# Gates and branch projections with tokens as rows, a DeltaNet inverse from 16-wide blocks, and a list schedule made in six passes

## The chip, the core and the metric

The kernel runs on one core of a Trainium2 chip. The metric is the time of one launch in microseconds of the device; lower is better. Five engines work side by side, each through a list of instructions of its own: TensorE (PE; its weight loads are shown apart as PEld), VectorE (DVE), ScalarE (ACT), GpSimd (POOL) and SyncE (SP), which here only issues DMA transfers.

## What is computed

Two layers over 256 tokens of width 1024. Each layer, cut to what matters here:

```python
h = rms_norm(x, norm_g)
proj = h @ w_in                        # qa ka va za ba aa | ub zb | qc kc vc zc iq ik iw | gates
ya = deltanet_branch(...)              # conv, silu, gated delta rule in chunks, per-head norm, silu(za)
yb = pooling_branch(ub, zb, pool_w, pool_scale)
yc = sparse_attention_branch(...)      # indexer scores, top 64 keys per query, softmax
projected = einsum('btnc,ncd->btnd', stack([ya, yb, yc]), w_branch)       # three of 512 x 1024
gate = sigmoid(gates.reshape(b, t, 3, 1024) + gate_b)
x = x + sum(gate * projected, axis=branch) @ w_out
```

Inside the DeltaNet branch a unit lower triangular matrix is inverted for each chunk and head (`triangular_solve(eye + lmat, eye)`). All is float32.

## The kernel before, in words

**Precision.** A float32 product is made of three products in the fp32r format: a weight block arrives by DMA in a buffer `raw` (4 of them), ACT casts it to `wh` (6 buffers), DVE subtracts to get `wl` (6 buffers), and TensorE adds up wh with hh, wh with hl and wl with hh, where hh and hl are the two parts of the normalised input. `wslot` (from line 576) does this for a block of 128 x 1024 numbers, so every block costs a DMA on SP, about a microsecond of ACT and 1.2 us of DVE.

**Projections.** `proj_cm` makes channels the rows of the result: the weights stand in TensorE, 256 tokens move past, 24 products of 128x256 per half bank. It serves the gates, the conv inputs and the silu paths. `proj_tm` makes tokens the rows: the activations stand and 512 weight columns move; it serves q, k and v of the attention. The results go to the PSUM banks `pj` (4 of them); `mx` (4 more) take the rest. The branch projections use the weights as stationary too, 256 tokens moving: the inner loops `for p in range(4)` after `acc`.

**Gates.** For each of the three branches four `proj_cm` of 256 channels, then ACT makes tanh with the bias `hb` of each channel's partition into a tile `tg`; DVE multiplies the branch product with it and adds into `acc`. `mh` and `ml`, the two parts of the sum, are the stationary side of the out-projection (`outp`, the first KOUT=2 of 8 row blocks for all output pieces, then the others piece by piece).

**Inverse.** `uc` holds the eight 32-wide diagonal blocks of both chunks and four heads. In 31 rounds DVE shuffles a row of `xi` into `xb`, multiplies and adds. Then TensorE joins 32-wide to 64-wide and 128-wide blocks with small products (p1, p2, p3), whose results ACT and DVE copy back.

**Order of the work.** Nothing is issued as it is written. Class `Plan` records every operation; `lay_out` is a list scheduler that walks through time with an estimated cost for each (`cost`), takes for each engine the ready operation of the smallest `prio` (the place in the program plus `plan.shift`: LATE, X1, CRIT and BACK are such shifts), and assigns buffers. `emit` then issues the list, so every instruction has one line in the profile, L454. The engines follow this list strictly in order on the chip.

**Parameters.** At the start and again at each layer SP issues small DMAs: `heads`, the norm gains, and into a tile `f` gate biases, conv weights, pool scales and one norm gain (77 rows), which TensorE transposes to channels as rows. `rsqrt` is a power on POOL (`rs` for the input norm, `r4k` and `r4q` for the attention's keys and queries, `rk`, `so` for the DeltaNet). After the input norm TensorE transposes `big` (the normalised x) and ACT and DVE make hh and hl from it.

Of the kernel before, what the change touches and what calls it, by code (L numbers as in the profile page):

```python
# [30 lines left out]
for _n, _c in (("ident", 128), ("upper", 128), ("supper", 128), ("strict", 128), ("bd", 128),  # L31
               ("ncaus", 128), ("eye32", 32), ("cosa", 128), ("sina", 128), ("cosi", 64),
               ("sini", 64), ("rcount", 64)):
    CST[_n] = (_w, _w + _c)
    _w += _c
CSTW = _w

NPAR = 77


LATE, X1, CRIT, BACK = 200, 132, ((-600, 60), (-600, -500)), 2000

KOUT = 2
NWARM = 40

# [3 lines left out]

PATIENCE = 600.0  # L50
NRAW, NSPL, NU, RU, WU, RB, RM, WM = 4, 6, 15, 3, 4, 1, 1, 6
# [4 lines left out]
def constants():  # L56
# [13 lines left out]
    put("eye32", (p % 32) == np.arange(32)[None, :])  # L70
# [58 lines left out]
class Tag:  # L129
    def __init__(self, phys, reserve, window, psum):  # L130
        self.phys, self.reserve, self.window, self.psum = phys, reserve, window, psum
        self.free = [(0.0, i) for i in range(len(phys))]
        self.order, self.next, self.parked, self.masks = [], 0, [], {}


class PTile:
    def __init__(self, tag):
        self.tag, self.slot, self.log, self.left, self.end = tag, None, [], 0, 0.0
        self.rank = None


class Op:
    __slots__ = ("eng", "call", "args", "kw", "cost", "tail", "prio", "port", "deps", "outs", "tiles", "wait", "est",
                 "start", "end", "n", "other", "turn", "weight")
# [24 lines left out]
class Plan:  # L169
# [3 lines left out]
    def __init__(self, tc):  # L173
        self.tc, self.nc, self.ops, self.shift = tc, tc.nc, [], 0
        nc = self.nc
        self.real = {"PE": nc.tensor, "DVE": nc.vector, "ACT": nc.scalar, "POOL": nc.gpsimd, "SP": nc.sync}
# [28 lines left out]
    def cost(self, eng, call, args, kw):  # L205
# [4 lines left out]
        if call == "dma_start":  # L210
            run = int(args[1].shape[-1]) * 4
            rate = 120.0 if run < 512 else 262.0 if run < 1024 else 318.0 if run < 4096 else 338.0
            return 475.0, n * out.shape[0] * 4 / rate, False
        if eng == "PE":
# [5 lines left out]
            if k <= 32:  # L220
                return 54.0, 170.0, False
            return 2 * (max(n, m) * (2.0 if k > 64 else 1.6) / 2.4 + 3), 170.0, False
# [10 lines left out]
        if eng == "POOL":  # L233
            if kw.get("op") == ALU.pow:
                return 400.0 + 155 * n, 40.0, True
# [18 lines left out]
    def add(self, eng, call, args, kw, other=None):  # L254
# [6 lines left out]
        o.prio, o.outs, o.est, o.start = o.n + self.shift, [], 0.0, None  # L261
# [21 lines left out]
        for t in o.tiles:  # L283
            if t.rank is None:
                t.rank = len(t.tag.order)
                t.tag.order.append(t)
        self.ops.append(o)
        return o

    def lay_out(self):  # L290
        import heapq

        for o in self.ops:
            o.wait = len(o.deps)
            for d in o.deps:
                d.outs.append(o)
            for t in o.tiles:
                t.left += 1
        engines = list(self.real)
        free = {e: 0.0 for e in engines}  # L300
        free["PE"] = 1000.0
# [4 lines left out]
        clock = Clock()  # L306
# [15 lines left out]
        def ready(o):  # L322
            at = slots(o)
            if at is not None:
                for e in [o.eng] + ([o.other[0]] if o.other else []):
                    heapq.heappush(soon[e], (max(o.est, at), o.prio, o.n, o.turn))
# [4 lines left out]
        def held(o, e):  # L331
            return o.other[2] if o.other and e == o.other[0] else o.cost

# [3 lines left out]
        def pick(e):  # L337
# [10 lines left out]
            if not now[e]:  # L348
# [4 lines left out]
                t, q = soon[e][0][0], soon[e][0][1:]  # L353
                if e in shared and uses(self.ops[q[1]], e):
                    t = max(t, shared["POOL" if e == "DVE" else "DVE"])
                return t, e, q
            if e not in shared:
                return t, e, now[e][0]
            blocked = shared["POOL" if e == "DVE" else "DVE"]
            q = now[e][0]  # L360
            if blocked <= t or not uses(self.ops[q[1]], e):
                return t, e, q
            room = blocked - t + SLACK
            for q2 in heapq.nsmallest(12, now[e]):
                if live(q2) and not uses(self.ops[q2[1]], e) and held(self.ops[q2[1]], e) <= room:
                    return t, e, q2
            return max(t, blocked), e, q
# [5 lines left out]
        while len(order) < len(self.ops):  # L373
# [20 lines left out]
            if max(got, o.est) > at + 1e-6:  # L394
# [4 lines left out]
                heapq.heappush(soon[e], (max(got, o.est), o.prio, o.n, o.turn))  # L399
# [3 lines left out]
            for t in o.tiles:  # L403
                if t.slot is None:
# [3 lines left out]
                    t.slot = f[1]  # L408
                    while g.next < len(g.order) and g.order[g.next].slot is not None:
                        g.next += 1  # L410
                    if g.free:
                        again, g.parked = g.parked, []
                        for p in again:
                            ready(p)
            o.start = at
            if e == "PE":
                free[e] = clock.run(at, o.cost, o.args[0].shape[0] * o.args[1].shape[0] / 16384.0)
# [5 lines left out]
            if o.call == "dma_start":  # L423
                dma_free = max(dma_free, at + 1360.0) + o.tail
# [24 lines left out]
    def emit(self):  # L449
# [3 lines left out]
        for o in self.lay_out():  # L453
# [5 lines left out]
def trunk(ctx: ExitStack, tc: tile.TileContext, x, norm_g, w_in, gate_b, conv_w, a_log, dt_bias, dn_onorm,  # L459
# [58 lines left out]
    cs = make("cs", [128, CSTW], F32)  # L518
# [5 lines left out]
    DMA.dma_start(x_sb[:, 1, :], x[0, 128:256, :])  # L524
    plan.shift = LATE
    DMA.dma_start(cs[:, 128:], cst[:, 128:])
# [7 lines left out]
    def brow(src_ap, n, name):  # L534
        t = make(name, [128, n], F32)
        DMA.dma_start(t, bass.AP(tensor=src_ap.tensor, offset=src_ap.offset, ap=[[0, 128], [1, n]]))
        return t

    heads = make("heads", [128, 2, 2, 4], F32)
    for i, a in enumerate((a_log, dt_bias)):  # L540
        DMA.dma_start(heads[:, i], bass.AP(tensor=a.tensor, offset=a.offset, ap=[[0, 128], [4, DEPTH], [1, 4]]))
    qkb = [brow(a, DEPTH * 128, n) for n, a in (("qn", q_norm), ("kn", k_norm))]
    qkn = [[b[:, l * 128:(l + 1) * 128] for b in qkb] for l in range(DEPTH)]
# [8 lines left out]
    sgr = make("sgr", [128, 128], F32R)  # L552
    V.tensor_copy(sgr, con("strict"))
# [13 lines left out]
    for i in range(2):  # L567
        G.memset(kiT[i], 0.0)

# [4 lines left out]
    def wslot(src, shape):  # L574
# [3 lines left out]
        for dst, s in ([(rv, src)] if not isinstance(src, list) else [(rv[:, :, a:b], s) for a, b, s in src]):  # L578
# [6 lines left out]
                lo[:, :n].rearrange("p (k c) -> p k c", k=shape[0]))  # L585

    for l in range(DEPTH):
# [12 lines left out]
        for t in range(2):  # L600
# [3 lines left out]
            ss = small(2, "ss")  # L604
            S.activation(fill(), xt[:, lo_], AF.Square, scale=1.0 / 32, accum_out=ss[:, 0:1])
            V.scalar_tensor_tensor(fill(), xt[:, hi_], 1.0 / D, xt[:, hi_], op0=ALU.mult, op1=ALU.mult,
                                   accum_out=ss[:, 1:2])
            se, rs = small(1, "se"), small(1, "rs")
# [8 lines left out]
            S.activation(xs[:, hi_], xg[:, hi_], AF.Copy, scale=rs)  # L617
# [17 lines left out]


        plan.shift = LATE
        rows = fill()[:, :128]
        DMA.dma_start(rows[0:24], gate_b[l].rearrange("i (r c) -> (i r) c", c=128))
        DMA.dma_start(rows[24:72], conv_w[l].rearrange("j (r c) -> (j r) c", c=128))  # L640
        DMA.dma_start(rows[72:76], pool_scale[l].rearrange("(r c) -> r c", c=128))
        DMA.dma_start(rows[76:77], dn_onorm[l:l + 1, :])
        pp = bank("mx")
        PE.transpose(pp[:, :NPAR], rows[:NPAR, :], ident[:NPAR, :NPAR])
        plan.shift = 0
        pt = make("pt", [128, NPAR], F32)
        S.copy(pt, pp[:, :NPAR])
        hb = make("hb", [128, 29], F32)
        V.tensor_scalar(hb[:, 0:24], pt[:, 0:24], 0.5, None, op0=ALU.mult)
        V.tensor_scalar(hb[:, 24:29], pt[:, 72:77], 0.5, None, op0=ALU.mult)  # L650
        tabs = []
        for i in range(2):
            c_t = make(f"tc{i}", [128, 2, 128], F32)
            s_t = make(f"ts{i}", [128, 2, 128], F32)
            for dst, name in ((c_t, "cosa"), (s_t, "sina")):
                tr = con(name).rearrange("p (t d) -> p t d", t=2)
                for t in range(2):
                    G.tensor_tensor(dst[:, t].rearrange("p (a d) -> p a d", a=2),
                                    tr[:, t, None, :].to_broadcast([128, 2, 64]),
                                    qkn[l][i].rearrange("p (a d) -> p a d", a=2), op=ALU.mult)  # L660
            tabs.append((c_t, s_t))
# [48 lines left out]
        def attend(which, c0):  # L710
            banks = proj_tm(c0)
            for t in range(2):
# [14 lines left out]
                rope(banks[t], t, tabs[0 if which == "q" else 1], ro)  # L727
# [189 lines left out]
        for which, c0, pr in (("k", KA, 0), ("q", QA, 0), ("k", KA, 1), ("q", QA, 1), ("v", VA, 0), ("v", VA, 1)):  # L917
# [3 lines left out]
            for b in range(2):  # L921
                blk = c0 // 128 + pr * 2 + b
                wc = [pt[:, 24 + j * 12 + blk:25 + j * 12 + blk] for j in range(4)]
# [18 lines left out]
        plan.shift = BACK  # L942
        ybh = make("y", [128, 4, T], F32R)
# [27 lines left out]
        for pr in range(2):  # L971
# [6 lines left out]
            for b in range(2):  # L978
                g = pr * 2 + b
                V.scalar_tensor_tensor(v2(y)[:, b], v2(ps)[:, b], hb[:, 24 + g:25 + g], zb[:, g], op0=ALU.mult,  # L980
# [3 lines left out]
        za = zgate(ZA)  # L984
# [9 lines left out]
        for c in range(2):  # L994
# [12 lines left out]
            if c == 0:  # L1007
# [4 lines left out]
                V.tensor_tensor(v4(kd), v4(ps), eg[:, 8:12, None].to_broadcast([128, 4, 128]), op=ALU.mult)  # L1012
# [25 lines left out]

        xi = make("xi", [128, 8, 32], F32)
        xb = make("xb", [128, 8, 32], F32)  # L1040
        V.tensor_copy(xi, con("eye32")[:, None, :].to_broadcast([128, 8, 32]))
        for r in range(31, 0, -1):
            n = 32 - r
            V.stream_shuffle(xb[:, :, r:], xi[:, :, r:], [r] * 32)
            V.tensor_tensor(xb[:, :, r:], xb[:, :, r:], uc[:, :, r:r + 1].to_broadcast([128, 8, n]), op=ALU.mult)
# [197 lines left out]
```

## Time and profile before

| | |
|---|---|
| median of 3 runs | 593.06 us (592.9 to 594.93) |
| the profiled execution's own time | 593.53 us |
| its span in the profile | 591.4 us |
| busy share of PE, DVE, ACT, POOL | 97%, 84%, 51%, 6% |
| mean granted clock of TensorE | 0.994 |
| moved by DMA | 95.66 MB, mean 162 GB/s |

The span is the time from the first to the last instruction; the rest of the execution's own time lies around it. A matmul's shown duration includes its way through the array, and the next one starts long before it ends, so what a stream of products costs is read from the distance between starts: the time of a stretch over the number of products in it. Idle time of an engine other than PE matters only where PE waits for it.

### The profile page before, as it was taken

The numbers are of one execution on the slowest core, as the hardware profiler recorded it, in microseconds if no ns is written. First come the engines' busy times: TensorE is split into PE (matmuls) and PEld (weight loads), VectorE is DVE, ScalarE is ACT, GpSimd is POOL, SyncE is SP. The second block draws the span as 40 slices with busy tenths as digits, with TensorE's granted clock in tenths as the row PEclk, the third lists the DMA queues.
The fourth block names the chain that finished last, engine by engine and source line by source line (L and its number), as shares of the span: only waits on it lengthen the run. The fifth ranks groups of instructions, "written<-read, shape, count | busy, mean of one in ns | idle before, by whom it ended". The sixth has DMA issues, their size and how long they took to land.

```text
span 591.4 us, 11398 instructions
## 1 busy us (share of the span) xinstructions
PE 575.8 (97%) x4423; PEld 546.5 (92%) x4423; DVE 495.7 (84%) x1122; ACT 301.3 (51%) x577; POOL 33.1 (6%) x36
## 2 busy tenths in 40 slices
PE   8899999999999999999989999999999999999997
PEld 6687999999899989999868879999999999999986
DVE  5899999999989975857587999999999998477571
ACT  6564376565365435545255635865554544435430
POOL 1011000011000021000011010000100002000000
PEclk9899999999999999999998999999999999999999
DMA  7662375676598653475445518927729865265511
GB/s 273 201 182 71 94 199 142 172 200 175 141 257 240 184 143 81 135 248 169 118 126 184 144 50 216 248 58 189 203 55 243 237 192 167 68 173 191 189 40 71
DMA packets 137313, 95.66 MB, mean 162 GB/s; under 512 B 5514, under 2 KB 128172, under 8 KB 137260
## 3 DMA queue, kind: packets, MB, share of 16 engines
q1 hardware_dynamic: 137260, 94.95, 56.5%
q8 instruction: 34, 0.56, 0.4%
q14 instruction: 19, 0.16, 0.1%
HBM read 93.89 MB, written 1.05 MB: 161 GB/s over the span
## 4 chain that ended last, share of the span: by engine, by line
PE 70%; DVE 19%; DMA 6%; ACT 2%; issue 2%; SPq 1%; ACTq 0%; DVEq 0%
PE pj L454 56%; PE mx L454 13%; DVE wl L454 5%; DVE u L454 5%; DMA raw<-in_w_in_dram 4%; DVE score L454 3%; DMA heads<-in_dt_bias_dram 1%; DVE top L454 1%; ACT wh L454 1%; SPq L454 1%; DVE y L454 1%; DVE big L454 1%; ACT u L454 0%; ACT hh L454 0%; DVE z L454 0%
## 5 line engine op out<-in xcount | busy, mean ns | idle before, releaser
L454 ACT CAST wh<-raw 128x1024 fp32r<-128x1024 f32 (+2 forms) x171 | 178.5, 1047 | 178.2 <-PE pj L454 86.1
L454 DVE TENSOR_TENSOR wl<-raw,wh 128x1024 fp32r<-128x1024 f32 (+1 forms) x174 | 210.3, 1214 | 36.4 <-ACT wh L454 35.1
L454 PE MATMUL pj<-hl,wh 128*128 128x256 f32 x832 | 120.8, 284 | 0.0
L454 PE MATMUL pj<-hh,wl 128*128 128x256 f32 x832 | 119.2, 284 | 1.5 <-DVE wl L454 1.5
L454 PE MATMUL pj<-hh,wh 128*128 128x256 f32 x832 | 120.6, 285 | 0.0
L454 PEld LDWEIGHTS pj<-hh,wl 128*128 128x128 f32 x832 | 107.8, 192 | 2.0 <-DVE wl L454 1.9
L454 PEld LDWEIGHTS pj<-hl,wh 128*128 128x128 f32 x832 | 108.7, 192 | 0.3
L454 PEld LDWEIGHTS pj<-hh,wh 128*128 128x128 f32 x832 | 108.5, 192 | 0.5
L454 PE MATMUL pj<-y,wh 128*128 128x256 f32 x384 | 54.7, 284 | 0.0
L454 PEld LDWEIGHTS pj<-y,wh 128*128 128x128 f32 x384 | 49.6, 192 | 0.2 <-DVE f L454 0.2
L454 PE MATMUL pj<-wh,hh 128*128 128x512 f32 (+1 forms) x128 | 38.7, 388 | 2.1 <-ACT hh L454 1.8
L454 PE MATMUL pj<-wh,hl 128*128 128x512 f32 (+1 forms) x128 | 39.0, 388 | 0.3 <-DVE hl L454 0.3
L454 PE MATMUL pj<-wl,hh 128*128 128x512 f32 (+1 forms) x128 | 37.7, 382 | 0.0
L454 PE MATMUL mx<-wh,y 128*128 128x512 f32 (+1 forms) x128 | 37.6, 377 | 0.0
L454 PE MATMUL mx<-u,u 128*128 128x128 f32 (+2 forms) x336 | 33.8, 249 | 1.2 <-DVE u L454 1.1
L454 PEld LDWEIGHTS mx<-u,u 128*128 128x128 f32 (+2 forms) x336 | 31.3, 165 | 2.5 <-DVE u L454 1.3
L454 DVE SCALAR_TENSOR_TENSOR u<-pj,pt,u 128x254 f32<-128x254 f32 (+2 forms) x72 | 31.3, 473 | 0.6 <-ACT u L454 0.6
L454 PE MATMUL pj<-y,wl 128*128 128x256 f32 x192 | 30.8, 283 | 0.0
L454 PEld LDWEIGHTS pj<-wh,hh 128*128 128x128 f32 x128 | 23.3, 192 | 6.6 <-ACT hh L454 2.4
L454 PEld LDWEIGHTS pj<-wh,hl 128*128 128x128 f32 x128 | 23.6, 193 | 5.1 <-DVE hl L454 1.4
L454 ACT COPY u<-mx 128x512 f32<-128x512 f32 (+2 forms) x30 | 12.6, 424 | 30.6 <-PE mx L454 25.9
L454 PEld LDWEIGHTS pj<-wl,hh 128*128 128x128 f32 x128 | 23.7, 194 | 4.2 <-DVE wl L454 0.2
(193 smaller groups left out, 688.6 us busy)
## 6 DMA issues: line engine op xcount, KB each, us to landing
raw<-in_w_in_dram SPq DMA_DIRECT2D x128, 512.0 KB, 4.5
raw<-in_w_branch_dram SPq DMA_DIRECT2D x24, 512.0 KB, 3.4
raw<-in_w_out_dram SPq DMA_DIRECT2D x16, 512.0 KB, 3.5
raw<-in_w_in_dram SPq DMA_DIRECT2D x4, 486.0 KB, 4.8
x_sb<-in_x_dram SPq DMA_DIRECT2D x2, 512.0 KB, 4.3
out_dram<-x_sb SPq DMA_DIRECT2D x3, 256.0 KB
raw<-in_w_in_dram SPq DMA_DIRECT2D x2, 324.0 KB, 4.1
cs<-in_cst_dram SPq DMA_DIRECT2D x1, 560.0 KB
```

Of the source, the lines that this page charges most:

```text
L454: getattr(self.real[o.eng], o.call)(*[put(a) for a in o.args], **{k: put(v) for k, v in o.kw.items()})
```

## The change

Five things change together.

1. *Gates and branch projections with tokens as rows.* `by_token` keeps a 128x128 block of hh, hl or of a branch's output standing and moves 512 weight columns, for two token blocks in turn, into two `pj` banks. A gate's bias now varies along the row, so `spread` loads it by a DMA that repeats one row to all 128 partitions (12 of 128x512), DVE adds it, and ACT makes tanh. The sum has tokens as rows, so 16 transposes per layer turn it for the out-projection.
2. *The inverse from 16-wide blocks.* 15 rounds instead of 31 on DVE, of up to 120 columns; then one more join on TensorE: `joined`, 32 products of 32x32 over the four row bands in turn, twice per layer.
3. *The schedule in passes.* `plan` lays the list out six times and keeps the shortest by its own reckoning. After each pass `deadlines` works out for each operation how late it may end without holding up TensorE in the order just found, and the other engines then rank by that time; TensorE keeps the program's rank. New rules: `SWITCH` and `REST` keep groups of small products apart, a small product is reckoned at 12 instead of 54 ns, an engine is kept off a PSUM bank that another is reading, some operations may not `begin` before a time.
4. *Parameter loads.* Conv weights, pool scales and norm gain of both layers are loaded once at the start and transposed once (128x106); these, `heads`, `qn`, most constants and `sgr` go through POOL's queue instead of SP's. SP issues the first weight block second.
5. *Constants of the order.* KOUT 2 to 4, BACK 2000 to 300, X1 and CRIT by a little; the gate `za` is made after the DeltaNet chain (`gated`); two DVE multiplications (`kd` and `rv`) go to ACT, in four pieces each.

```diff
-LATE, X1, CRIT, BACK = 200, 132, ((-600, 60), (-600, -500)), 2000
-KOUT = 2
+LATE, X1, CRIT, BACK = 200, 138, ((-600, 0), (-600, -500)), 300
+KOUT = 4
+SWITCH = 90.0
+REST = 2500.0
+LATER = 18000.0
+PASSES = 6
...
             if k <= 32:
-                return 54.0, 170.0, False
+                return 12.0, 170.0, False
...
+    def plan(self):
+        best, time = None, 1e18
+        for i in range(PASSES):
+            order = self.lay_out()
+            if self.time < time:
+                time = self.time
+                best = [(o, o.eng, o.call) for o in order], [(t, t.slot) for g in self.tags for t in g.order]
+            self.deadlines(order)
...
+        def rank(o, e):
+            return o.prio if e == "PE" or o.late is None else o.late
...
+            if e == "PE" and not small and t < whole + REST and fill(self.ops[now[e][0][1]]) < 0.3:
+                for q in heapq.nsmallest(40, now[e]):
+                    if live(q) and fill(self.ops[q[1]]) > 0.9:
+                        return t, e, q
...
+    for l in range(DEPTH):
+        r0 = l * NPAR
+        G.dma_start(rows[r0:r0 + 48], conv_w[l].rearrange("j (r c) -> (j r) c", c=128))
+        G.dma_start(rows[r0 + 48:r0 + 52], pool_scale[l].rearrange("(r c) -> r c", c=128))
+        G.dma_start(rows[r0 + 52:r0 + 53], dn_onorm[l:l + 1, :])
...
-        for r in range(31, 0, -1):
+        for r in range(15, 0, -1):
...
+        def joined(lhs, rhs):
+            ps = bank("mx")[:, :256].rearrange("p (n j) -> p n j", n=8)
+            for i in range(8):
+                for bs in bands:
+                    mm(ps[bs, i], lhs[bs, i], rhs[bs, i], True, True)
+            return ps
+
+        S.copy(z32, joined(um, xt))
+        V.tensor_tensor(xi, joined(z32, xi), xi, op=ALU.add)
...
+        def by_token(w, k_all, sides):
+            banks = [bank("pj"), bank("pj")]
+            for k0 in range(0, k_all, 2):
+                wh, wl = wslot(w[:, k0:k0 + 2], (2, 512))
+                seq = [(wx, side, kw) for wx, side in ((wh, 0), (wh, 1), (wl, 0)) for kw in range(2)]
+                for n, (wx, side, kw) in enumerate(seq):
+                    for t in range(2):
+                        mm(banks[t], sides[side][:, k0 + kw, t * 128:(t + 1) * 128], wx[:, kw, :],
+                           k0 + n == 0, k0 + n == k_all + 3)
+            return banks
...
+                bias = make("tg", [128, 512], F32)
+                spread(DMA, bias, gate_b[l, i, cols])
+                banks = by_token(wi[:, :, GT + i * D + half * 512:GT + i * D + (half + 1) * 512], KB, (hh, hl))
+                tg = [make("tg", [128, 512], F32), bias]
+                for t in range(2):
+                    V.tensor_tensor(tg[t], banks[t], bias, op=ALU.add)
+                    S.activation(tg[t], tg[t], AF.Tanh, scale=0.5)
```

How often each product is issued, before and now: 128x256 products of the projections of h, 832 three times and now 448 three times; of the branches, 384 and 192 and now none; 128x512 products of h, 96 three times and now 288 three times; of the branches, none and now 192 and 96; transposes of `big`, 56 and now 88; 32x32 products, 80 and now 208.

Three places show how the order moves. The first is TensorE in layer 0 around the inverse's joins (`xi`, `um` and the `u` tiles beside them belong to the inverse, `hh`, `hl`, `wh` and `wl` to a projection that fills the time). Before:

```order
L454 MATMUL pj_118<-hl_80,wh_71 128x256 x8
L454 MATMUL pj_118<-hh_79,wl_73 128x256 x5
L454 MATMUL mx_122<-u_96,u_99 32x32 x8
L454 MATMUL mx_120<-u_96,u_101 32x32 x8
L454 MATMUL pj_118<-hh_79,wl_73 128x256 x3
L454 MATMUL mx_119<-u_108,xi_195 32x32 x4
```

Now:

```order
L542 MATMUL pj_118<-wh_69,hl_80 128x512
L542 MATMUL mx_120<-u_105,um_136 32x32 x32
L542 MATMUL pj_115<-wh_69,hl_80 128x512
...
L542 MATMUL pj_115<-wh_70,hh_79 128x512
L542 MATMUL mx_122<-xi_197,u_105 32x32 x32
L542 MATMUL pj_118<-wh_70,hl_80 128x512
```

Where a row of 16 products stood, two of 32 come ahead of it, with 11 products of 512 columns between the two.

The second is the start, on the two queues that issue DMAs. SP before, from its fifth DMA on (`f` takes the parameters, `raw` the weights):

```order
L454 DMA raw_63<-in_w_in_dram 128x2x512
...
L454 DMA cs_124<-in_cst_dram 128x1120
L454 DMA heads_125<-in_a_log_dram 128x8
L454 DMA heads_125<-in_dt_bias_dram 128x8
L454 DMA qn_126<-in_q_norm_dram 128x256
L454 DMA kn_127<-in_k_norm_dram 128x256
L454 DMA f_94<-in_gate_b_dram 24x128
L454 DMA f_94<-in_conv_w_dram 48x128
L454 DMA f_94<-in_pool_scale_dram 4x128
L454 DMA f_94<-in_dn_onorm_dram 1x128
L454 DMA raw_63<-in_w_in_dram 128x3x324
```

SP now has three transfers between the first four weight blocks and the next, and POOL, between the powers `rs` and `r4k`, has eleven:

```order
L542 DMA raw_65<-in_w_in_dram 128x2x512
L542 DMA raw_66<-in_w_in_dram 128x2x512
L542 DMA cs_124<-in_cst_dram 128x450
L542 DMA kn_126<-in_k_norm_dram 128x128
L542 DMA tg_89<-in_gate_b_dram 128x512
L542 DMA raw_63<-in_w_in_dram 128x3x324
```

```order
L542 TENSOR_TENSOR rs_145<-se_143,mhalf_130 128x1
L542 MEMSET big_113 128x4x16
L542 DMA heads_127<-in_dt_bias_dram 128x8
L542 DMA rows_129<-in_conv_w_dram 48x128
...
L542 DMA sgr_128<-in_cst_dram 128x128
L542 DMA cs_124<-in_cst_dram 128x528
L542 DMA heads_127<-in_a_log_dram 128x8
L542 DMA qn_125<-in_q_norm_dram 128x256
L542 TENSOR_TENSOR r4k_154<-se_152,mhalf_130 128x4
```

The parameters of `f` are gone from SP; POOL's `r4k` now stands behind eleven DMAs instead of behind none.

The third is DVE at the border of the two layers, from the sum `se` of the second token block to the scaling of `big` that TensorE's transposes wait for. Before and now:

```order
L454 TENSOR_SCALAR se_139<-ss_137 128x1
L454 TENSOR_TENSOR wl_74<-raw_65,wh_67 128x1024
L454 TENSOR_TENSOR wl_75<-raw_66,wh_72 128x996
L454 TENSOR_TENSOR wl_77<-raw_63,wh_69 128x996
L454 TENSOR_TENSOR u_101<-pj_118,tc_146 128x512
L454 TENSOR_SCALAR hb_143<-pt_142 128x24
L454 TENSOR_SCALAR big_112<-big_112,rs_141 128x512
```

```order
L542 TENSOR_SCALAR se_143<-ss_141 128x1
L542 TENSOR_TENSOR wl_76<-raw_65,wh_68 128x1024
L542 TENSOR_SCALAR big_113<-big_113,rs_145 128x512
L542 TENSOR_TENSOR wl_77<-raw_66,wh_69 128x996
L542 TENSOR_TENSOR wl_78<-raw_63,wh_70 128x996
L542 TENSOR_TENSOR hl_80<-mx_122,hh_79 128x4x128
```

Five operations stood between the two, and now one.

## Rows read from the trace of the kernel before

**Rows 1.** The page: instructions and span, busy time of each engine, and the clock that TensorE was granted in 40 equal slices of the span (in tenths; 9 is full).

```profile
span 591.4 us, 11398 instructions
PE 575.8 (97%) x4423; PEld 546.5 (92%) x4423; DVE 495.7 (84%) x1122; ACT 301.3 (51%) x577; POOL 33.1 (6%) x36
PEclk9899999999999999999998999999999999999999
```

**Rows 2.** The chain of work that ended last, its pieces in order of time: start, us, what, number of instructions.

```profile
5.97 8.78 DMA heads<-in_dt_bias_dram
14.77 3.37 DMA raw<-in_w_in_dram
...
228.60 1.33 PE mx L454 x12
...
279.21 17.73 PE mx L454 x78
```

**Rows 3.** Waits of PE, by what it waited for: us in total, times, the longest.

```profile
PE mx L454 <- DVE u L454: 2.3, 3, 1.1
PE mx L454 <- DVE big L454: 2.2, 2, 1.9
PE pj L454 <- ACT hh L454: 1.8, 1, 1.8
PE mx L454 <- DMA f<-in_pool_scale_dram: 1.6, 1, 1.6
PE pj L454 <- DVE wl L454: 1.5, 2, 1.3
PE mx L454 <- ACT big L454: 1.2, 2, 0.8
PE mx L454 <- POOL wh L454: 1.1, 1, 1.1
...
```

**Rows 4.** Three stretches: from:to and length in us, then busy us (instructions) of PE, PEld, DVE, ACT and POOL, the granted clock as a share, the DMA engines' busy share, GB/s.

```profile
22.07:25.47 3.40, 3.32 (x8) 2.65 (x9) 3.40 (x11) 2.23 (x8) 0.00 (x0) 0.50 0.02 5
154.00:210.00 56.00, 56.00 (x467) 56.00 (x468) 52.90 (x134) 27.92 (x35) 0.00 (x0) 1.00 0.82 226
312.20:315.59 3.39, 3.36 (x11) 2.16 (x9) 2.40 (x5) 1.02 (x3) 0.22 (x1) 0.50 0.34 129
```

**Rows 5.** PE in order of time, at the inverse of layer 0: start, us from the first instruction's start to the last one's end, the group, in brackets the idle time before it and what ended it.

```profile
211.90 0.89 PE L454 MATMUL mx<-u,u 32*32 32x32 f32 x32 [1.10 <-DVE u L454]
212.72 0.62 PE L454 MATMUL pj<-hh,wl 128*128 128x256 f32 x3
...
214.00 0.47 PE L454 MATMUL mx<-xi,u 32*32 32x32 f32 x13
214.40 0.86 PE L454 MATMUL pj<-hh,wh 128*128 128x256 f32 x5
```

**Rows 6.** PE likewise, at the border of the layers.

```profile
309.04 0.26 PE L454 MATMUL mx<-cs,f 77*128 77x77 f32 x1 [1.61 <-DMA f<-in_pool_scale_dram]
311.23 1.30 PE L454 MATMUL mx<-cs,big 128*128 128x128 f32 x8 [1.93 <-DVE big L454]
```

**Rows 7.** DVE in order of time, at the same border.

```profile
302.36 0.68 DVE L454 TENSOR_TENSOR x_sb<-x_sb,mx 128x512 f32<-128x512 f32 x1
...
304.09 0.69 DVE L454 SCALAR_TENSOR_TENSOR f<-x_sb 128x512 f32<-128x512 f32 x1
...
305.31 0.21 DVE L454 TENSOR_SCALAR se<-ss 128x1 f32<-128x1 f32 x1
305.44 2.32 DVE L454 TENSOR_TENSOR wl<-raw,wh 128x1024 fp32r<-128x1024 f32 x2
308.90 1.20 DVE L454 TENSOR_TENSOR wl<-raw,wh 128x996 fp32r<-128x996 f32 x1 [1.14 <-ACT wh L454]
...
310.69 0.48 DVE L454 TENSOR_SCALAR big<-big,rs 128x512 f32<-128x512 f32 x1
```

**Rows 8.** SP in order of time, at the start: the issue of DMAs.

```profile
4.57 0.87 SPq L454 DMA_DIRECT2D cs<-in_cst_dram  x1
...
13.55 0.23 SPq L454 DMA_DIRECT2D f<-in_dn_onorm_dram  x1
13.99 2.24 SPq L454 DMA_DIRECT2D raw<-in_w_in_dram  x4
```

**Rows 9.** POOL in order of time, at the start and at the border of the layers.

```profile
7.50 0.56 POOL L454 TENSOR_TENSOR rs<-se,mhalf 128x1 f32<-128x1 f32 x1 [1.70 <-DVE se L454]
...
27.18 1.01 POOL L454 TENSOR_TENSOR r4k<-se,mhalf 128x4 f32<-128x4 f32 x1 [19.02 <-DVE se L454]
...
305.60 1.47 POOL L454 TENSOR_TENSOR rs<-se,mhalf 128x1 f32<-128x1 f32 x1 [9.83 <-DVE se L454]
```

**Rows 10.** POOL by groups of the same shape: instructions, then busy us in all and mean ns of one, then idle time before them.

```profile
L454 POOL TENSOR_TENSOR rk<-ssk,mhalf 128x4 f32<-128x4 f32 x4 | 8.0, 1989 | 154.0 <-DVE ssk L454 154.0
L454 POOL TENSOR_TENSOR so<-so,mhalf 128x4 f32<-128x4 f32 x4 | 4.0, 1007 | 30.3 <-DVE so L454 30.3
```

**Rows 11.** DVE by groups likewise.

```profile
L454 DVE TENSOR_TENSOR u<-pj,ts 128x512 f32<-128x512 f32 x8 | 5.5, 684 | 1.1 <-ACT u L454 1.1
L454 DVE CAST wh<-raw 128x1024 fp32r<-128x1024 f32 x3 | 2.1, 690 | 3.7 <-PE pj L454 3.7
```

**Rows 12.** One stretch, DVE's work on the tile `xb` of layer 0's inverse alone: from:to and length in us, busy us (instructions), clock, DMA share, GB/s.

```profile
62.00:211.00 149.00, 27.59 (x124) 1.00 0.68 184
```

More of the change, by code (lines that the diff above doesn't have):

```diff
@@ L131, in __init__, with clear @@
         self.phys, self.reserve, self.window, self.psum = phys, reserve, window, psum
-        self.free = [(0.0, i) for i in range(len(phys))]
-        self.order, self.next, self.parked, self.masks = [], 0, [], {}
+        self.order, self.masks = [], {}
+        self.clear()
+    def clear(self):
+        self.free = [(0.0, i) for i in range(len(self.phys))]
+        self.next, self.parked, self.held = 0, [], {}
 class PTile:
     def __init__(self, tag):
-        self.tag, self.slot, self.log, self.left, self.end = tag, None, [], 0, 0.0
-        self.rank = None
+        self.tag, self.log, self.rank, self.ops = tag, [], None, 0
+        self.clear()
+    def clear(self):
+        self.slot, self.left, self.end, self.reader, self.until, self.then = None, self.ops, 0.0, "", 0.0, None
 class Op:
     __slots__ = ("eng", "call", "args", "kw", "cost", "tail", "prio", "port", "deps", "outs", "tiles", "wait", "est",
-                 "start", "end", "n", "other", "turn", "weight")
+                 "start", "end", "n", "other", "turn", "late", "own", "begin")
 class Clock:
@@ L283, in add @@
         for t in o.tiles:
+            t.ops += 1
             if t.rank is None:
@@ L414, in lay_out @@
                             ready(p)
+            if e in ("DVE", "ACT"):
+                for z in o.tiles:
+                    if z.tag.psum:
+                        z.reader, z.until = e, at + o.cost + o.tail + 36.0
             o.start = at
             if e == "PE":
-                free[e] = clock.run(at, o.cost, o.args[0].shape[0] * o.args[1].shape[0] / 16384.0)
+                part = fill(o) < 0.3
+                free[e] = clock.run(at, o.cost + (SWITCH if part != small else 0.0), fill(o))
+                if small and not part:
+                    whole = at
+                small = part
             else:
@@ L634, in trunk @@
         plan.shift = 0
[L637 to L661, printed above, removed]
+        if l == 0:
+            prepare(0, "k")
+            plan.shift = LATE
+            prepare(0, "q")
+            plan.shift = 0
+        pt, hb = pts[:, l], hbs[:, l]
         def proj_cm(c0):
```

277 lines of the change are left out of this document (185 added, 92 removed).

## Prediction

> **What bounds the kernel now.** I read the page first, then the chain of work that ended last, then TensorE's waits, and last the order of time around each wait. PE is busy for 97% of the span, and the granted clock is full in nearly every slice [rows 1]. The chain shows long pieces of PE alone; in the first 18 us DMA stands in it, too [rows 2]. [...] So the time is TensorE's stream of products, plus some 15 us that lie in a few places: the start, the border of the layers, two spots at the DeltaNet. DVE is nearly as full, 52.90 of 56.00 us in the stretch of gates and inverse, and PE waits for nothing there [rows 4]: work taken from DVE is worth only what it shortens in a wait. Everything is therefore priced on PE's path.
>
> **The change part by part.** The sum is made against the profiled execution's own 593.53 us, which is 0.1% above the median of 593.06.
>
> *Gates and branches.* 832 − 448 = 384 products of 256 columns go three times, and all 576 of the branches: 1728. There come 576 + 288 = 864 of 512 columns. A stretch of almost nothing but 256-column products has 467 in 56.00 us, 119.9 ns each [rows 4]; the stretch of 78 products of the out-projection, 512 columns, takes 17.73 us, 227.3 ns each [rows 2]. 1728 × 119.9 = 207.2 us against 864 × 227.3 = 196.4: **−10.8 us**. A moving row twice as long pays the fixed part half as often.
>
> *Turning the sum.* 32 transposes of 128x128 come. Twelve small full-array steps in the chain take 1.33 us, 111 ns each [rows 2]: **+3.6 us**, in PE's order and so on its path.
>
> *Joins of the inverse.* 128 products of 32x32 come, in four groups of 32. Each product leaves two records (16 products in the order, 32 records in the row), and that group takes 0.82 us from its start to the next one's, 25.6 ns per record with the way in and out; it works in two row bands [rows 5]. For a group of 64 records that gives 1.64 us, 6.6 for four: the upper bound. At the end of the small products 13 records stand 0.40 us long, 31 ns each, in the same band one after the other [rows 5]; if four bands each kept that spacing side by side, a record would cost 7.7 ns, 0.49 us a group, 2.0 in all: the lower bound. The new groups go over four bands where the row has two, so I take half the upper bound: **+3.3 us**. [...]
>
> *The inverse's rounds.* DVE spends 27.59 us per layer on `xb` [rows 12]; 15 of 31 rounds, shorter ones at that, leave 13.4 at most, so DVE loses at least 28.4 us over two layers. It gets 24 bias additions of about 0.68 (+16.4, by the group with a bank and a tile as inputs) and seven more casts of `wh` of 0.69 (+4.8) [rows 11], and loses four multiplications to ACT. The net is a few us of relief. It is priced at nothing, since PE does not wait in that stretch [rows 4]. If DVE were late, the first join would be; 11 products of 512 columns, 2.5 us, cover the step between the two joins.
>
> *Bias loads.* 12 DMAs of 256 KB. The DMA engines are busy 0.82 of the time in the stretch where gates run, at 226 GB/s [rows 4]; 3.1 MB more are some 14 us of that rate, spread over two layers of which 18% is free (10 us in this stretch alone). Nothing on the path; if the cover were gone, ACT's cast of the next block would be late by 1.1 us a load.
>
> *Border of the layers.* PE's wait of 1.6 us for `pool_scale` goes, since no parameter is loaded there [rows 3, 6]: **−1.6**. The wait of 1.93 for `big` comes from DVE: after `se` it does three `wl`, the third after waiting for ACT 1.14 us, and only at 310.69 scales `big` [rows 6, 7]. Now one `wl` stands between. The chain then is: addition 0.68, square sum 0.69, `se` 0.21, `rs` 1.47, scaling 0.48, and a `wl` of 1.2 [rows 7, 9], 4.7 us; 21 products of 512 columns stand on PE against it, 4.8 us. I leave 0.7 of the wait: **−1.2**. With both waits mostly gone, PE no longer has the thin stretch from 307 to 311 that came before the half clock at 312 [rows 4, 6]: **−1.7**.
>
> *Start.* SP spends 4.57 to 13.99 issuing twelve transfers before the fifth weight block [rows 8], whose landing at 18.14 stands in the chain [rows 2], and after it ACT's cast and then `hh`, for which PE waits 1.8 us [rows 3]. With three transfers left the block comes some us earlier: **−1.8**. Half clock near 22 follows that gap; I count half of it: **−0.9**.
>
> *Waits for `wl` and `u` at the DeltaNet* (1.3 and 1.1 [rows 3]): the ranking by due times is meant for these; half: **−1.2**. New places with little cover (the joins, the turned sum just before the out-projection): **+1.0**.
>
> *KOUT, BACK, `gated`, the two multiplications on ACT* move work that PE does not wait for; ACT is busy 27.92 of 56 us [rows 4] and covers it.
>
> PE's work −10.8 + 3.6 + 3.3 = −3.9; waits and clock −1.6 − 1.2 − 1.7 − 1.8 − 0.9 − 1.2 + 1.0 = −7.4. Sum −11.3: **582 us**. Its own range is 576 to 588.
>
> **The rivals.**
>
> *The waits stay.* The passes take their due times from the same estimated costs; at the border the plan's times were wrong because a DMA came late, and six passes would repeat that. Then only PE's work and the `pool_scale` wait go: 593.5 − 3.9 − 1.6 = 588.0, with joins at their upper bound 591.3; about 589. For it: the waits are few and each has its own cause. Against it: two of the causes (parameter DMAs ahead of weights, three `wl` ahead of `big`) are gone from the order itself.
>
> *Nearly every wait goes.* All 11.7 us but the 1.1 at the very start, and both half-clock stretches, 14.0 us: 593.5 − 3.9 − 14.0 = 575.6, with joins at the lower bound 574.
>
> *POOL's queue stops the start (slower).* `r4k` now stands behind eleven DMA issues, where before it followed `rs` with nothing long between. The keys' scaling needs `r4k`, PE's transposes of the keys need that, and behind PE stands everything. POOL is free at 7.50 + 0.56 = 8.1 us, and `r4k` ran at 27.18 [rows 9]; some 3 us earlier is wanted if the start gets shorter, 24.5. Eleven issues fit if each takes under 1.5 us. On SP an issue takes 0.23 to 0.87 [rows 8], which would fit. POOL's own operations take up to twice as long beside a busy DVE, 1989 against 1007 ns for the same shape [rows 10]; 0.87 doubled is 1.7, and `r4k` would be 2.7 us late, some 585. At 3.5 us each it is late by 22: 604. It turns the sign to slower above 2.8 us per issue. [...]
>
> **How the numbers follow.** A measurement of this kernel can tell about 0.5% from no change, 590.1 to 596.0 us against 593.06. Forecast 0.54, all of it faster; waits stay 0.25, of which 0.11 below 590.1 and 0.14 above; nearly every wait goes 0.09, faster; POOL's queue 0.12, slower. Faster 0.74, same 0.14, slower 0.12. The range reaches from 574, the lower bound of the best case, to 592, the upper bound of the case in which the waits stay; what it leaves out is the slower rival and a little at either edge.
>
> **What would show each step.** Products of 512 columns for gates 227 ns apart from start to start; groups of 64 records of 32x32 in 0.5 to 1.6 us; no wait of PE for a parameter DMA; the granted clock full near 312; `big` scaled within 5.1 us of the last addition; no wait for `hh` near 20; `r4k` on POOL at 25 us or earlier. Wrong: POOL's `r4k` far behind its `se`, with PE waiting for a `u` tile near 30; new waits of PE at the joins; or the sum of PE's waits still above 9 us.

## The result and the profile after

| | before | changed |
|---|---|---|
| median | 592.98 us (4 runs, 592.14 to 594.93) | 578.56 us (4 runs, 578.17 to 578.61) |
| ratio | | 0.9751, 95% interval 0.9727 to 0.9775 |
| profiled execution, its span | 593.53, 591.4 us | 578.55, 576.4 us |

The changed kernel is 2.5% faster; the forecast was 582 us, with 574 to 592 as its range. The span fell by 15.0 us, the prediction's sum by 11.3. A few executions take over 1.5% longer than the fastest of the same kernel, at a lower granted clock (612.71 us at 0.965 against 603.34 at 0.986 in part 1 alone); medians and ratios here and below leave them out.

The page of the changed kernel, the lines that answer to [rows 1]:

```profile
span 576.4 us, 10225 instructions
PE 566.5 (98%) x3846; PEld 504.1 (87%) x3846; DVE 484.8 (84%) x1026; ACT 297.0 (52%) x574; POOL 35.6 (6%) x47
PEclk9999999999999999999999999999999999999999
```

No slice is below 9 tenths of the clock any more: both stretches at half clock of [rows 4] are gone. The waits of PE, against [rows 3]:

```profile
PE mx L542 <- ACT u L542: 1.3, 1, 1.3
PE mx L542 <- POOL wh L542: 1.1, 1, 1.1
PE pj L542 <- DVE hl L542: 1.1, 2, 0.6
PE pj L542 <- ACT hh L542: 0.9, 1, 0.9
PE mx L542 <- ACT kiT L542: 0.9, 1, 0.9
PE mx L542 <- DVE u L542: 0.8, 2, 0.5
PE pj L542 <- ACT wh L542: 0.3, 1, 0.3
PE mx L542 <- DMA u<-in_norm_g_dram: 0.2, 1, 0.2
```

They come to 6.6 us, where all of before came to 12.3 (the 11.7 of the rows and two of 0.3). The waits for `pool_scale` and for `big` at the border are not among them; the two longest new ones (ACT `u`, ACT `kiT`) are where nothing was forecast.

PE at the joins of layer 0 and at the branch products with tokens as rows, in order of time (start, length of the group, count):

```profile
190.69 0.74 PE L542 MATMUL mx<-u,um 32*32 32x32 f32 x64 [0.29 <-DVE u L542]
191.36 0.97 PE L542 MATMUL pj<-wh,hl 128*128 128x512 f32 x3
...
194.08 0.75 PE L542 MATMUL mx<-xi,u 32*32 32x32 f32 x64
194.77 1.20 PE L542 MATMUL pj<-wh,hl 128*128 128x512 f32 x4
...
263.98 1.98 PE L542 MATMUL pj<-wh,y 128*128 128x512 f32 x8
265.79 0.85 PE L542 MATMUL pj<-wl,y 128*128 128x512 f32 x3
266.48 1.04 PE L542 MATMUL mx<-cs,big 128*128 128x128 f32 x8
267.27 0.47 PE L542 MATMUL pj<-wl,y 128*128 128x512 f32 x1
```

From start to start a group of 64 records takes 0.67 to 0.69 us, 10.6 ns per record; eight products of 512 columns take 1.81 us, 226 ns each; eight transposes 0.79, 99 ns each.

The border, DVE and then POOL of the changed kernel, against [rows 7, 9]:

```profile
297.57 0.21 DVE L542 TENSOR_SCALAR se<-ss 128x1 f32<-128x1 f32 x1
297.70 1.22 DVE L542 TENSOR_TENSOR wl<-raw,wh 128x1024 fp32r<-128x1024 f32 x1
299.37 0.48 DVE L542 TENSOR_SCALAR big<-big,rs 128x512 f32<-128x512 f32 x1 [0.45 <-POOL rs L542]
```

```profile
297.87 1.47 POOL L542 TENSOR_TENSOR rs<-se,mhalf 128x1 f32<-128x1 f32 x1 [7.07 <-DVE se L542]
```

`big` is scaled 1.8 us after `se`, where it was 5.4; now DVE waits 0.45 us for POOL's `rs`, not PE for DVE. And the start on POOL, the place of the slower rival:

```profile
10.62 0.74 POOL L542 DMA_DIRECT2D heads<-in_dt_bias_dram  x1
...
16.76 0.55 POOL L542 DMA_DIRECT2D qn<-in_q_norm_dram  x1
23.06 3.84 POOL L542 TENSOR_TENSOR r4k<-se,mhalf 128x4 f32<-128x4 f32 x1 [5.75 <-DVE se L542]
```

Eleven issues are done at 17.3 us, each 0.5 to 0.7; then POOL waits for DVE's `se`. `r4k` was not held up by the queue, but itself takes 3.84 us.

### The profile page after: what moved, and what is told of

Same layout as the page of the kernel before. It is cut to its first block, busy times and chain, and to the rows that moved or that the text cites. A ratio compares the mean times of both kernels' runs of the same rounds, so it can differ in the third digit from the quotient of the medians.

```text
span 576.4 us, 10225 instructions
## 1 busy us (share of the span) xinstructions
PE 566.5 (98%) x3846; PEld 504.1 (87%) x3846; DVE 484.8 (84%) x1026; ACT 297.0 (52%) x574; POOL 35.6 (6%) x47
## 4 chain that ended last, share of the span: by engine, by line
PE 82%; DVE 11%; issue 2%; ACT 2%; DMA 2%; POOL 1%; SPq 0%; DVEq 0%; ACTq 0%; POOLq 0%
PE pj L542 64%; PE mx L542 18%; DVE wl L542 4%; DVE u L542 3%; DVE big L542 1%; DMA x_sb<-in_x_dram 1%; DMA raw<-in_w_in_dram 1%; POOL r4k L542 1%; ACT u L542 1%; ACT wh L542 0%; DVE hl L542 0%; DVE y L542 0%; DVE tg L542 0%; POOL rk L542 0%; DVE wh L542 0%
## 5 line engine op out<-in xcount | busy, mean ns | idle before, releaser
L542 ACT CAST wh<-raw 128x1024 fp32r<-128x1024 f32 (+1 forms) x164 | 171.5, 1048 | 169.3 <-PE pj L542 117.8
L542 PE MATMUL pj<-wh,hh 128*128 128x512 f32 (+1 forms) x320 | 91.0, 388 | 0.9 <-ACT hh L542 0.9
L542 PE MATMUL pj<-wh,hl 128*128 128x512 f32 (+1 forms) x320 | 90.0, 386 | 1.1 <-DVE hl L542 1.1
L542 PE MATMUL pj<-wl,hh 128*128 128x512 f32 (+1 forms) x320 | 90.2, 385 | 0.0
L542 PEld LDWEIGHTS pj<-wh,hh 128*128 128x128 f32 x320 | 58.6, 188 | 11.9 <-ACT hh L542 1.3
L542 PE MATMUL pj<-hh,wh 128*128 128x256 f32 x448 | 64.4, 285 | 0.3 <-ACT wh L542 0.3
L542 PE MATMUL pj<-hl,wh 128*128 128x256 f32 x448 | 64.3, 284 | 0.0
L542 PE MATMUL pj<-hh,wl 128*128 128x256 f32 x448 | 63.6, 284 | 0.0
L542 PEld LDWEIGHTS pj<-hh,wh 128*128 128x128 f32 x448 | 58.3, 192 | 0.8 <-ACT wh L542 0.5
L542 PEld LDWEIGHTS pj<-hl,wh 128*128 128x128 f32 x448 | 58.1, 192 | 0.0
L542 PE MATMUL pj<-wh,y 128*128 128x512 f32 (+1 forms) x208 | 51.9, 384 | 0.0
```

Source lines behind the costliest of these rows:

```text
L542: getattr(self.real[o.eng], o.call)(*[put(a) for a in o.args], **{k: put(v) for k, v in o.kw.items()})
```

## Experiments

All times are medians; beside each, the kernel before ran on the same chip (593.4 to 593.9 there), and ratios are to those runs.

**Part 1 alone** (gates and branches with tokens as rows, in the kernel before; `by_token`, `spread` and the turned sum exactly as in the diff above, all else untouched).

> The kernel before with part 1 alone: gates and branch projections with tokens as rows, the sum turned by 32 transposes; inverse, scheduler and parameter loads as before. If the parts add up as priced on TensorE's path, 593.0 - 10.8 + 3.6 = 585.8 us, with the waits of before (11.7 us) still there. If the bias loads, the 24 additions on VectorE and the turned sum bring waits of their own, 589 or more, with new waits of PE for big, tg or y tiles between 210 and 300 us.

Measured: 607.35 us, ratio 1.0229 (1.0173 to 1.0284). Slower than before by 14 us, further out than the rival said. PE of this kernel ahead of the third branch in layer 0:

```profile
266.04 1.12 PE L454 MATMUL pj<-hh,wl 128*128 128x256 f32 x8
270.76 1.65 PE L454 MATMUL pj<-wh,y 128*128 128x512 f32 x3 [3.60 <-ACT y L454]
```

```profile
270.76:276.40 5.64, 5.64 (x13) 4.41 (x14) 1.39 (x3) 1.66 (x2) 0.00 (x0) 0.50 0.22 89
```

The second row is the stretch right behind the wait (length, busy us of the engines, clock, DMA share, GB/s): 3.60 us of waiting are followed by 5.64 at clock 0.50, so the wait costs 6.4, not 3.6. The 256-column products ahead of it are the projection of `za`, and `y` is made from it: nothing is left on PE between the two. BACK = 2000 counts recorded operations, and the program has 832 products fewer, so the same number should push `za` further back among the gates; that the count is the reason, and not the place of `za` in the program, was not tried apart.

The two waits for `y` are not all. PE's waits come to 19.9 us, 7.6 more than before, and a mean clock of 0.974 over 605.5 us means some 16 us lost at half clock (an estimate; before, the two stretches lost 3.4). From 200 to 300 us the mean clock is 0.91. The longest stretch at half clock, 10.24 us at 0.50 from 222.04 on, with PE busy throughout, lies elsewhere: behind the small products of the inverse and two waits of 0.38 and 0.47.

**Part 3 alone** (the classes `Tag` to `Plan` of the changed kernel in the kernel before, with SWITCH, REST and PASSES).

> The kernel before with the new list scheduler alone (six passes, ranks by due time, small groups apart, the new costs), nothing else. TensorE's work is that of before. If the waits went because of the ranking by due times, PE's waits fall from 11.7 to about 6 us and one half-clock stretch goes: 586 to 588 us, with the wait for pool_scale (1.6) left. If they went because of the other order of loads and the edits in the program, it stays at 592 to 594.

Measured: 587.88, ratio 0.9891 (0.9853 to 0.9930). The new scheduler alone mends waits: PE's are 6.1 us, with 2.0 for `pool_scale` still there. Which of its rules does it, this run doesn't tell.

**The changed kernel with the old inverse.**

```diff
-        for r in range(15, 0, -1):
+        for r in range(31, 0, -1):
...
-        S.copy(z32, joined(um, xt))
-        V.tensor_tensor(xi, joined(z32, xi), xi, op=ALU.add)
```

> The changed kernel with the inverse of before: 31 rounds from 32-wide blocks on VectorE, and no joins of 32 products. If the relief of VectorE is worth nothing, the joins' price comes back: 578.6 - 3.1 = 575.5 us (the joins took 4 x 0.68 us from start to start and 0.09 us each to get in). If VectorE is what the stretch depends on, its 14 us more per layer make PE wait for u ahead of the 32- and 64-wide products: 580 us or more.

Measured: 576.13, ratio 0.9707 (0.9690 to 0.9723): faster than the changed kernel by 2.4 us. The stretch 154 to 240 us, this kernel and then the changed one (columns as in [rows 4]):

```profile
154.00:240.00 86.00, 86.00 (x506) 72.76 (x505) 81.46 (x206) 40.44 (x49) 0.00 (x0) 1.00 0.69 214
```

```profile
154.00:240.00 86.00, 85.70 (x675) 73.16 (x674) 70.24 (x164) 41.68 (x86) 2.31 (x3) 1.00 0.58 175
```

DVE is busy 81.46 of 86 us with the old inverse and PE all 86.00: the 11 us that the shorter rounds save are no one's wait in this stretch. The joins come on top. Over the whole of this execution (577.73 us, the longest of its four) PE's waits are 8.2 us against the changed kernel's 6.6, so the list differs elsewhere too.

**The changed kernel with one pass** (`PASSES = 6` to `PASSES = 1`).

> The changed kernel with one pass instead of six, so that the list is the first pass's: ranks by place in the program, no due times; all else as changed. If the due times bring the fall of the waits, PE's waits come back by 4 to 6 us: 582 to 585 us. If the edits in the program (loads, shifts, gated) bring it, 578 to 580.

Measured: 592.64, ratio 0.9983 (0.9960 to 1.0006): all of the change but the passes is no faster than before, and both expectations were too low. PE's waits are 15.7 us, 9.1 more than with six passes, and behind the longest of them six products of 256 columns take 1.41 us from start to start, 235 ns each, where eight ahead of it took 0.96, 120 each; the granted clock is 0.97 over the first 100 us (0.994 over 590.6 us: some 3.5 us lost, an estimate). The longest wait, on PE:

```profile
65.51 1.12 PE L542 MATMUL pj<-hh,wl 128*128 128x256 f32 x8
72.49 1.08 PE L542 MATMUL mx<-cs,u 128*128 128x128 f32 x4 [5.86 <-DVE u L542]
```

and DVE there, a few of its rows, in this kernel and then in the changed one:

```profile
63.50 0.61 DVE L542 MAX8 top<-score 128x8 f32<-128x256 f32 x2
...
71.60 0.42 DVE L542 MAX8 top<-score 128x8 f32<-128x256 f32 x1
71.94 0.41 DVE L542 TENSOR_TENSOR u<-u,u 128x256 f32<-128x256 f32 x1
...
72.72 0.69 DVE L542 TENSOR_TENSOR u<-pj,tcq 128x512 f32<-128x512 f32 x1
```

```profile
56.45 0.69 DVE L542 TENSOR_TENSOR u<-pj,tcq 128x512 f32<-128x512 f32 x1 [0.33 <-ACT u L542]
...
61.37 0.76 DVE L542 TENSOR_TENSOR u<-u,u 128x256 f32<-128x256 f32 x2
...
63.36 0.30 DVE L542 MAX8 top<-score 128x8 f32<-128x128 f32 x1
```

By place in the program the sixteen top-k rounds come ahead of the rotation of the queries, for which PE stands still; by due time the rotation goes first, as the mask of the top-k is needed much later.

**Parts 1 and 3** (both edits above together).

> The kernel before with parts 1 and 3: gates and branches with tokens as rows, and the new scheduler; BACK stays 2000, the gate za where it was, inverse and loads as before. Theory: the two waits of 3.6 us for y and the half clock behind them come from TensorE's own order (BACK counts operations, the program now has fewer, so za's projection is moved behind all gates), which the passes leave as it is; then PE still waits for y twice and the time is 588 to 593 us. Rival: they came from late work on VectorE and ScalarE, which due times mend: 587.9 - 7.2 = 580.7 us.

Measured: 588.35, ratio 0.9900 (0.9832 to 0.9968). The time is the theory's, its two waits for `y` half so: PE ranks by place in every pass, and in layer 1 it still waits 3.47 us for `y`; in layer 0 a transpose in front of the same products waits 2.64 for `u`. The longest of PE's waits in all:

```profile
PE mx L539 <- DVE u L539: 4.2, 3, 2.6
PE pj L539 <- ACT y L539: 3.7, 2, 3.5
```

**Parts 1 and 3 with `za` ahead of the third branch's gates.**

```diff
-LATE, X1, CRIT, BACK = 200, 132, ((-600, 60), (-600, -500)), 2000
+LATE, X1, CRIT, BACK = 200, 132, ((-600, 60), (-600, -500)), 300
...
-        za = zgate(ZA)
...
+            if n == 2:
+                gated()
```

> As the run of parts 1 and 3, with za made ahead of the third branch's gates (gated) and BACK at 300. Theory: no wait for y, and the parts add up: 587.9 - 10.8 + 3.6 = 580.7 us (579 to 583). Rival: without the new loads and KOUT the waits at the border and the start are larger than that: 584 or more.

Measured: 574.02, ratio 0.9649 (0.9593 to 0.9704). No wait for `y`, and 4.5 us faster than the whole change, 6.7 below the sum that the theory gave: PE's waits are 5.8 us here, and the border's is 0.8 for a DMA, not 1.6. Part of the 6.7 is the base: part 3 alone ran from 583.61 to 588.66, and from its profiled execution, the 583.61, the sum is 576.4.

**The same under the scheduler of before.**

> Part 1 with za ahead of the third branch's gates and BACK at 300, under the scheduler of before. Theory: only the waits for y go from the run of part 1 alone (7.1 us and 5 to 6 us of half clock): 593 to 596 us, still no faster than before, because VectorE and ScalarE serve the wrong bank first. Rival: with za in place the priced 7.2 us come out: 585 to 588.

Measured: 593.78 (five of ten executions, 585.76 to 594.30), ratio 0.9962 (0.9909 to 1.0014): no change that can be told, though the best execution lies in the rival's range. In the profiled one, 590.54, the waits for `big` (2.5 and 2.1), `u` (2.0), `hh` (1.6) and a parameter DMA (1.8) stand about as before, and a mean clock of 0.985 over 588.8 us loses some 9 us (an estimate), more than the 3.4 of before.

Four runs together say the most. Part 3 alone takes 5.6 us off, part 1 with `za` early alone nothing, both together 19.6. So `za` in place is worth 14 us under either scheduler, and part 3 as a whole 20 once the work is cheaper (593.8 to 574.0). Without part 3 the cheaper work shows no gain, and without the cheaper work part 3 shows 5.6 of its 20.

**The joins' products band by band.**

```diff
-            for i in range(8):
-                for bs in bands:
+            for bs in bands:
+                for i in range(8):
```

> The changed kernel with the joins' products in another order: eight in one row band, then eight in the next, instead of the four bands in turn. Theory: a band works one product at a time, 31 ns per record, and bands side by side are what makes a group of 64 records 0.68 us; now a group takes about 1.6 to 2.0 us, +1.0 to +1.3 each, 4 to 5 us in all: 582.5 to 584. Rival: the array takes a small product every 10.6 ns whatever its band: 578.6.

Measured: 583.11, ratio 0.9807 (0.9740 to 0.9873); +4.6 us on the changed kernel. PE at the first join of layer 0:

```profile
189.65 1.88 PE L542 MATMUL mx<-u,um 32*32 32x32 f32 x64 [0.28 <-DVE u L542]
191.46 0.97 PE L542 MATMUL pj<-wh,hl 128*128 128x512 f32 x3
```

1.81 us instead of 0.67: 28 ns per record against 10.6. The order over the four bands in turn makes the joins cheap.

**Parameter loads on SP** (all of part 4's `G.dma_start` but `sgr` to `DMA.dma_start`).

> The changed kernel with its parameter loads on SP's queue instead of POOL's (all but sgr, which is cast on its way): POOL has one DMA ahead of r4k where there were eleven. Theory: POOL's issues took 0.5 us each and were done 6 us before r4k was wanted, so only the first r4k can change; 577.5 to 579, the same as changed within 1 us. Rival: the queue on POOL costs what the change lacks against the run of parts 1 and 3 with za early (574.0), beyond the joins: 576 to 577, with r4k at 1 us instead of 3.84 and PE's wait of 0.54 for u near 27 gone. Rival on the other side: ten more issues between SP's weight blocks make weights late, 581 or more.

Measured: 579.53, ratio 0.9777 (0.9749 to 0.9804): the same within the interval. `r4k` still takes 2.70 us on POOL with no DMA near it, so the queue isn't what stretches it (last section).

**KOUT 4 on the run of parts 1 and 3 with `za` early.**

> Parts 1 and 3 with za early (574.0 us) and KOUT 4 instead of 2, nothing else. Theory: KOUT only moves when the pieces of the out-projection end; PE's waits at the border there are 0.8 us for a DMA and 0.7 for big, of which some goes: 573 to 574.5. Rival: four blocks of the out-projection ahead need their weights and the turned sum earlier and the last pieces end closer together: 575 or more.

Measured: 573.93, ratio 0.9673 (0.9653 to 0.9692): the same as without.

**The changed kernel with the old inverse and the loads on SP.**

> The changed kernel with the inverse of before and the parameter loads on SP's queue: both together. What is left of the change over the run of parts 1 and 3 with za early is the single parameter load, KOUT 4, two multiplications on ScalarE and the small shifts. Theory: the inverse's joins and a little of POOL's queue are all that the change lacks: 574 to 575. Rival: something else in it costs 2 us: 576 or more, as with the old inverse alone (576.1).

Measured: 575.90, ratio 0.9715 (0.9691 to 0.9740): the rival, as with the old inverse alone. What the change lacks by 2 us beside the joins is neither POOL's queue nor KOUT.

**The new inverse on top of parts 1 and 3 with `za` early and KOUT 4.**

> Parts 1 and 3 with za early and KOUT 4 (573.9 us), and now the inverse from 16-wide blocks on top: the mirror image of the run that took it out of the changed kernel. Theory: the joins cost TensorE 3.1 us and the shorter rounds of VectorE give nothing back: 577.0 (576 to 578). Rival: in this base, with all constants' loads and the two multiplications still on the old queues, VectorE is the nearer bound and its relief pays: 574 or less.

Measured: 581.18, ratio 0.9811 (0.9773 to 0.9850): 7.3 us slower, more than the joins' 3.1. In its profiled execution the span is 577.8 us against 572.3: the joins' 3.1, and transposes near 143 and 424 us that now wait for an `f` tile from DVE, 2.1 in all. It is a new list, not only four groups more; why this list is the worse was not followed further.

## Why the prediction was right, and where it was off

**What bounds it.** Right. TensorE's stream plus a dozen microseconds of waits (11.7 in [rows 3]) and two stretches at clock 0.50 (3.40 and 3.39 us in [rows 4], of which half, 3.4, is lost) was the whole of it: all three fell, and DVE was no bound even at 81.46 of 86 us, as the old inverse in the changed kernel shows.

**Gates and branches, −10.8.** 226 ns per 512-column product, against the 227.3 read from [rows 2]. As work on TensorE the term holds; as a gain by itself it does not. Alone it made the kernel slower by 14 us, with 7.6 us more of waits and some 12 more lost at half clock. The sum adds parts as if the order of all else stayed; that it came out all the same has, as far as can be told, to do with its being read from the final order, in which the passes and the place of `za` were already fitted to the new work. In that there is luck: with one pass the same edits end at 592.6, outside the range.

**KOUT, BACK, `gated`, the two multiplications, 0.** Right for KOUT in the run that tried it (573.9 against 574.0). Wrong for BACK and `gated`, said to "move work that PE does not wait for": `za` early, by the two together, is worth 14 us once part 1 is in (588.4 to 574.0).

**Turning the sum, +3.6.** 32 transposes of 88 to 99 ns, about 3.0; the row of twelve [rows 2] held other small products too.

**Joins, +3.3.** 4 × 0.68 from start to start, and 0.09 each in the product ahead of a group: 3.1. Half the upper bound was close, and the reason for it, four bands where the rows had two, is borne out by the run that takes the bands one after the other. In the changed kernel a record takes 10.6 ns, and with the bands one after the other 28.

**The rounds, 0.** Right: with the old inverse back DVE works 11 us more in the stretch and PE loses nothing there. Part 2 is a loss of 2.4 us in this kernel.

**Border, −1.2 and −1.6.** Both waits went wholly (−1.9 and −1.6); one of 0.6 for `hl` came. **Clock, −2.6.** Both stretches went, −3.4. **Start, −1.8.** PE's waits in the first 40 us fell from 4.9 to 3.2, near the term, but by other waits than it names: the one for `hh` is now 0.9, near 10 us, two for `big` (1.2) are gone, and `hl` and `u` cost 0.5 each. Between the fourth and the fifth weight block there were nine transfers, not the twelve of the prediction; the fifth is now issued from 7.76 us on instead of 13.99. **Other waits, −1.2 + 1.0.** Better than that: the waits of [rows 3] for `u` fell by 1.5 and for `wl` wholly (1.5); new are 1.3 for ACT `u` and 0.9 for `kiT`. The first has a cause in the trace, PE and then ACT of the changed kernel:

```profile
142.88 0.98 PE L542 MATMUL mx<-y,wl 128*128 128x256 f32 x6 [1.25 <-ACT u L542]
```

```profile
141.44 0.36 ACT L542 ACTIVATE u<-mx,eg 128x128 f32<-128x128 f32 x1
...
141.94 0.89 ACT L542 ACTIVATE u<-mx,eg 128x128 f32<-128x128 f32 x3
```

The four pieces of the `kd` multiplication (`u<-mx,eg`), which the prediction called covered on ACT, read a bank of `mx`; they end at 142.83, and PE's next product into `mx` starts then. **Bias loads, 0.** Right: no wait of PE or DVE for a `tg` from DMA, and the DMA engines' share from 154 to 240 us is 0.58.

The ledger: work −10.8 + 3.0 + 3.1 = −4.7, waits −5.7, clock −3.4, in all −13.8 of the 15.0. With 226 ns for the 864 products, 195.3 us, the gates would be −11.9 and the whole −14.9; that pace was read from single groups, so this is an estimate.

**The rivals.** "The waits stay" was wrong in its reason: six passes did not repeat the first one's list, and with one pass the waits do not stay, they grow (15.7 us, 592.6). The passes decide the result in this kernel; I gave them 1.2 us by name. "POOL's queue" fell at its deciding number, 0.5 to 0.7 us per issue against 1.5; of its path a wait of 0.5 us for `u` near 27 is left. "Nearly every wait goes" was met by no run; parts 1 and 3 with `za` early reach its 574, but without the joins and with 5.8 us of waits.

**Open.** Why the changed kernel without the joins is still 2 us above parts 1 and 3 with `za` early. Its longest waits lie at `hl`, `y`, `u` and `kiT`; two pieces of the change were not tried apart (`kd` and `rv` on ACT, the single parameter load with its own transpose ahead of `kiT`).

## What to carry to other kernels

Price the work of a part on the engine that bounds, but do not add up the gains of parts where a scheduler lays all of them out: build the parts alone and in pairs, since one that saves 7 us of work cost 14 by moving what others wait for. Look again, after such an edit, at what was placed by counting operations. Work taken from an engine that nobody waits for is worth nothing, however full it is. And let the other engines rank by due times taken from the bounding engine's order: here the edits to the work gave nothing until the scheduler was changed with them, and the best runs of all (574.0 and 573.9) left out parts 2 and 4.

## What the runs showed of the hardware

In part 1 alone a wait of 3.60 us cost 6.4, since the 5.64 us behind it ran at 0.50 of the clock and so lost half its length, 2.8 (an estimate). The length of a wait alone does not tell what it costs: the two waits at the border, 1.6 and 1.9 us, were followed by 3.4 us at half clock in the kernel before, and nearly the same two (1.8 and 1.8) by 6.8 in part 1 alone, where the mean clock from 300 to 400 us is 0.97; the waits of the changed kernel, none above 1.3, brought no such stretch (mean clock 0.999), nor did one of 1.7 for `y` in the kernel with the old inverse, where the mean clock is 1.000.

In these two runs POOL's small power `r4k` ends with DVE's subtractions, not after a time of its own. DVE in the changed kernel and then with the loads on SP:

```profile
22.88 3.12 DVE L542 TENSOR_TENSOR wl<-raw,wh 128x664 fp32r<-128x664 f32 x3
26.93 0.69 DVE L542 TENSOR_TENSOR u<-u,r4k 128x512 f32<-128x512 f32 x1 [0.94 <-POOL r4k L542]
```

```profile
22.95 1.98 DVE L542 TENSOR_TENSOR wl<-raw,wh 128x664 fp32r<-128x664 f32 x2
25.87 0.69 DVE L542 TENSOR_TENSOR u<-u,r4k 128x512 f32<-128x512 f32 x1 [0.94 <-POOL r4k L542]
```

With three `wl` in a row it takes 3.84 us, with two 2.70, and both times it ends 0.9 us after the last of them. In the kernel before it took 1.01 [rows 9], where it started 0.28 us ahead of a pair of `wl`. A busy DVE alone does not stretch a power so: in the kernel before DVE was busy all through the four `rk` of [rows 10], which took 1.82 to 2.44 us, but all through the four `r4q` too, which took 1.01 each; where the prediction speaks of twice the time beside a busy DVE, only the first four bear it out. In both runs above DVE then waited 0.94 us for `r4k`. That its own `wl` made the power late is the reading that fits these two; what holds POOL up meanwhile was not shown.
